# Where an MLP block's shared products are added, which engine empties a turning block, and from which pool a chunk takes its bank, in a two-layer fp32 decoder on Trainium2

## The chip, the cores and the metric

The kernel runs on one core of one Trainium2 chip. Its metric is the time of one execution in device microseconds. TensorE (PE) does the matmuls into PSUM, VectorE (DVE) and ScalarE (ACT) read PSUM and work on SBUF, GpSimd (POOL) here issues the DMAs that add to their destination, and SyncE (SP) issues the loads. Each engine takes its instructions in order and waits on semaphores.

## The reference

Two layers on x of 512 tokens by 1024, in fp32. The final norm follows the second.

```python
h = rmsnorm(x, g_mix)
z = h @ w_in            # attention q, k, v | retention q, k, v, g | gate_a | gate_b
A = sliding-window attention, window 128, 8 query heads on 2 kv heads, rotary, sinks
B = chunkwise retention, 4 heads, rms norm per head, swish gate
x = x + (sigmoid(gate_a) * (A @ w_a) + sigmoid(gate_b) * (B @ w_b)) @ w_out
h2 = rmsnorm(x, g_mlp)
x = x + square(relu(h2 @ w_up)) @ w_down        # 1024 -> 4096 -> 1024
out = rmsnorm(x, g_final)                        # after layer 2
```

## The kernel before

**Products.** Every fp32 operand is split into a high and a low part that TensorE can multiply (`hi` by ACT at L308, `lo` by DVE at L309), and each product is three matmuls, high by high, high by low, low by high (`products`, L354 to L356). A matmul has 128 weights by 512 or 256 columns.

**Weights.** They stream in units of 128 x 1024 through five `raw` buffers (`raw_tile`, L170). SP issues the loads four units ahead, and a unit is split three units before its matmuls (`unit`, `split_until`). For some units DVE first adds two loaded halves (L267 for `pair`, L290 for `block`). Which units are needed and when is a fixed list; the order of all instructions is laid out by a scheduler when the program is built.

**The mix part of a layer** multiplies xh, xl (the split input) by `w_in` in chunks of 128 columns. A `group` (L400) computes four chunks at once, here k, v, q(0), q(1), and then come q(2) and q(3) by `chunk` (L388, called at L652 and L653), each into a bank of PSUM, after which `rotate` (L566 to L572, ACT and DVE) reads the bank. PSUM has eight banks: five in the pool `ps_mm`, three in `ps_aux`. Between the parts POOL also sums blocks of weights in DRAM with accumulating DMAs (`sum_steps`).

**The MLP part** runs over eight blocks of 512 hidden columns a layer. Both matrix products of a block are computed with seven half-size multiplications in place of eight. `pair` (L1138, called twice a block) makes the hidden values: seven multiplications of twelve 128 x 256 matmuls into three banks a, e, b, with ACT copies between them (L1152, L1154, L1157) and relu, square, split and sums on ACT and DVE. `down` (L1213) makes the block's share of y: seven multiplications of two times twelve 128 x 512 matmuls. Its banks are a[0..1] and c[0..1] from `ps_mm` and b[0..1] from `ps_aux`. In order:

- a: first product; ACT copies a into b.
- c: product, then `into.early(1, 1, m, c[m], -1)`.
- b += product, then `into.early(0, 1, m, b[m], 1)`.
- a += product, `put(0, 0)`; c += product, `put(0, 1)`; b += product, `put(1, 1)` with sign -1; b += product, `put(1, 0)`.

Here (i, j) is a quarter of y (half i of the columns, half j of the tokens) and m one of two 128-token parts. So the quarters (1,1) and (0,1) are the sum of an early share and a later one.

**Where the shares go.** For blocks 0 to 6 `into` is `Adding`. Its `early` and `put` both call `send` (L1274): ACT scales the bank by the token's norm factor into a temporary (L1276), and POOL issues a DMA that adds the temporary to y in DRAM (L1278). That is twelve sends of 256 KB a block, four of `eu` from `early` and eight of `y` from `put`. For block 7 `into` is `Ending`: y's quarters are read back into SBUF (L1292), and DVE adds each share from the bank in place (`add`, L1307); only the early (1,1) shares go by ACT and an accumulating DMA. In layer 0, block 7 is then turned back into x (`turn`, L1329; `carry`, L1354, for the halves i = 1, within the next layer's first group). In layer 1, `put` of block 7 goes on to the final norm: ACT's sum of squares (L1315), DVE's multiplication by the gain (L1316, every part), and when both halves of a token part are there, its scaling by 1/rms, for i = 1 by DVE (L1323), for i = 0 by ACT (L1326), and the stores of the result. The last block of layer 1 uses `down_plain` (L1181), which has no early shares.

All temporaries (`temp`: eu, y, rot, junk and others) share one ring of seven 128 x 512 tiles (L131): a new one waits until the tile seven before it is read for the last time, which for a sent tile is the landing of its DMA.

Of the kernel before, what the change touches and what calls it, by code (L numbers as in the profile page):

```python
# [12 lines left out]
AF = mybir.ActivationFunctionType  # L13
ALU = mybir.AluOpType
# [4 lines left out]
T = 512  # L19
# [95 lines left out]
def decoder(ctx, tc, xT, x_first, w_in, w_a, w_b, w_out, w_up, w_pair, w_down, w_end, tables, decay, band, g_last, out):  # L115
    nc = tc.nc
# [7 lines left out]
    ps_mm = ctx.enter_context(tc.tile_pool(name="ps_mm", bufs=5, space=PSUM))  # L124
    ps_aux = ctx.enter_context(tc.tile_pool(name="ps_aux", bufs=3, space=PSUM))

    def f32(ap):
        return ap.bitcast(F32)

    def temp(name="t"):  # L130
        return tmp.tile([P, T], F32, tag="t", name=name, bufs=7)  # L131

    def big(name, dtype=F32):
        return tmp.tile([P, 2, T], dtype, tag="big", name=name, bufs=6)

    def bank(pool, name):
        return pool.tile([P, T], F32, tag=pool.name, name=name)
# [177 lines left out]
    def unit(name, layer):  # L315
        i = state["next"]
        assert order[i][:2] == (layer, name), (order[i], layer, name)
        state["next"] += 1
        split_until(i + SPLIT + 1)
        return parts.pop(i)  # L320
# [27 lines left out]
    def products(ps, pairs, start, stop, resume=False):  # L348


        n = len(pairs)
        for i, ((ah, al), (bh, bl)) in enumerate(pairs):
            more = {"skip_group_check": True} if resume else {}
            nc.tensor.matmul(ps, ah, bh, start=start and i == 0, stop=False, **more)  # L354
            nc.tensor.matmul(ps, ah, bl, start=False, stop=False, **more)  # L355
            nc.tensor.matmul(ps, al, bh, start=False, stop=stop and i == n - 1, **more)  # L356
# [10 lines left out]
    xs = [(xh[:, k, :], xl[:, k, :]) for k in range(KD)]  # L367
# [4 lines left out]
    def advance(rate=1.0):  # L372

        credit[0] += rate
        while credit[0] >= 1.0:
            credit[0] -= 1.0
            while background:
                try:
                    next(background[0])
                    break  # L380
                except StopIteration:
                    background.pop(0)
# [2 lines left out]
        while background:  # L385
            advance()

    def chunk(name, layer, moving, evacuate, rate=1.0):  # L388

        hi, lo = unit(name, layer)  # L390
        n = len(moving)
        ps = bank(ps_mm, "mm")
        pairs = [((hi[:, k * P : (k + 1) * P], lo[:, k * P : (k + 1) * P]), moving[k]) for k in range(n)]
        advance(rate)
        products(ps, pairs[: n // 2], True, False)
        advance(rate)
        products(ps, pairs[n // 2 :], False, True)
        evacuate(ps)
# [110 lines left out]
    def scaled_input(k, which):  # L509

        split(xh[:, k, :], xl[:, k, :], x[:, k, :], gain[:, which * KD + k : which * KD + k + 1])

    def squared_input(k, which):
        if k == 0:
            acc_of[which] = tmp.tile([P, T], F32, tag="acc", name="acc", bufs=1)
        square_sum(acc_of[which], x[:, k, :], k == 0)
# [32 lines left out]
    def layer_body(layer):  # L549
# [14 lines left out]
        def rotate(ps, tabs, early=False):  # L564
            a, b = temp("rot"), temp("rot2")
            nc.scalar.activation(b[0:64, :], ps[64:128, :], AF.Copy)  # L566
            nc.scalar.activation(b[64:128, :], ps[0:64, :], AF.Copy)
            if early:
                nc.scalar.activation(a, ps, AF.Copy)
            nc.vector.tensor_tensor(a, a if early else ps, tabs[0], ALU.mult)  # L570
            nc.vector.tensor_tensor(b, b, tabs[1], ALU.mult)
            nc.vector.tensor_tensor(a, a, b, ALU.add)  # L572
            return a
# [20 lines left out]
        def beside(g, stack, src):  # L594
            for s in range(2):
                own, other = 64 * s + 32 * g, 64 * s + 32 - 32 * g
                nc.sync.dma_start(f32(stack)[other : other + 32, :], f32(src)[own : own + 32, :])
# [33 lines left out]
        def put_q(c):  # L631
            def put(ps):
                r = rotate(ps, attn_tabs, layer == 0 and c < 2)
                if c % 2 == 0:
                    qlo[:] = [big("qlo")]
                lo = qlo[0][:, c % 2, :]
                for g in range(N_KV):
                    nc.scalar.activation(q_s[g][:, c, :], r, AF.Copy)
                nc.vector.tensor_tensor(lo, r, f32(q_s[0][:, c, :]), ALU.subtract)
                for g in range(N_KV):  # L640
                    beside(g, q_s[g][:, c, :], lo)

            return put
# [6 lines left out]
            {0: squares, 1: rms_mix.prepare, 2: stats} if layer == 0 else {0: carried.pop(), 2: rms_mix.prepare, 3: stats},  # L650
        )
        chunk("w_in", layer, xs, put_q(2))  # L652
        chunk("w_in", layer, xs, put_q(3))  # L653
        turn_v()

        a_t = [slots.four() for _ in range(2)]
# [187 lines left out]
        class Head:  # L844


            def __init__(self, h):
                self.h = h
# [110 lines left out]
        for u in range(4):  # L959
            hi, lo = unit("w_a", layer)  # L960
            for j in range(2):
                c = 2 * u + j
                ps = bank(ps_mm, "mm")
# [78 lines left out]
        last = layer == DEPTH - 1  # L1042
        y = dram.tile([P, NB, D], F32, name=f"y{layer}")
# [7 lines left out]
        factor, negative = (columns[:, i * NB : (i + 1) * NB] for i in range(2))  # L1051
        if last:
# [3 lines left out]
            last_gain = gain_tile[:, 0:2, :]  # L1056
# [199 lines left out]
        class Adding:  # L1256


            def __init__(self, e):
                self.e = e  # L1260

            def last_but_one(self):
                pass
# [2 lines left out]
                pass  # L1266

            def early(self, i, j, m, ps, sign):
                self.send(i, j, m, temp("eu"), ps, sign, last or self.e > 0)

            def put(self, i, j, m, ps, sign):
                self.send(i, j, m, temp("y"), ps, sign, last or self.e > 0 or j == 1)

            def send(self, i, j, m, t, ps, sign, add):  # L1274
                block = 2 * j + m
                nc.scalar.activation(t, ps, AF.Copy, scale=(factor if sign > 0 else negative)[:, block : block + 1])  # L1276
                how = {"accum_op": ALU.add} if add else {}
                nc.gpsimd.dma_start(y[:, block, i * T : (i + 1) * T], t, **how)  # L1278

        class Ending:  # L1280


            def __init__(self):
                self.y, self.done = {}, set()
                for i, j in ((1, 1), (0, 1), (0, 0), (1, 0)):
                    if last:
                        two = x[:, 4 * j + 2 * i : 4 * j + 2 * i + 2, :]
                    elif i == 0:
                        two = late_box[0][:, 2 * j : 2 * j + 2, :]
                    else:  # L1290
                        two = big("y")
                    nc.gpsimd.dma_start(two, y[:, 2 * j : 2 * j + 2, i * T : (i + 1) * T])  # L1292
                    for m in range(2):
                        self.y[i, j, m] = two[:, m, :]
# [13 lines left out]

            def put(self, i, j, m, ps, sign):
                block = 2 * j + m  # L1310
                self.add(i, j, m, ps, (factor if sign > 0 else negative)[:, block : block + 1])
                if last:
                    v = self.y[i, j, m]
                    first, total, both = (sq[:, n * NB + block : n * NB + block + 1] for n in range(3))
                    nc.scalar.activation(temp("junk"), v, AF.Square, accum_out=both if i else first)  # L1315
                    nc.vector.tensor_tensor(v, v, last_gain[:, i, :], ALU.mult)  # L1316
                    if not i:
                        nc.vector.tensor_scalar(first, first, 1.0 / D, EPS, ALU.mult, ALU.add)
                        return
                    nc.scalar.activation(total, both, AF.Sqrt, bias=first, scale=1.0 / D)  # L1320
                    nc.vector.reciprocal(total, total)
                    v = self.y[1, j, m]
                    nc.vector.tensor_scalar(v, v, total, None, ALU.mult)  # L1323
                    nc.sync.dma_start(out[:, block, T:], v)
                    v = self.y[0, j, m]
                    nc.scalar.activation(v, v, AF.Copy, scale=total)  # L1326
                    nc.scalar.dma_start(out[:, block, :T], v)
# [24 lines left out]
                    carried.append(self.carry)  # L1352

            def carry(self):  # L1354
                for half in range(2):
                    for j in (1, 0):
                        self.turn(1, j, half, ps_aux)
                    for k in (4 + 2 * half, 5 + 2 * half):
                        scaled_input(k, g_mix + 2)
                for k in range(KD):  # L1360
                    squared_input(k, g_mix + 2)
                    nc.sync.dma_start(spill[:, k, :], x[:, k, :])
                late_box[0] = late_tile(F32R)
                slots.add(late_box[0])
# [200 lines left out]
```

## Time and profile before

| | |
|---|---|
| median of three executions | 1502.52 us (1497.24 to 1502.98) |
| profiled execution | 1501.42 us |
| its span, first to last instruction | 1499.7 us |
| mean granted TensorE clock | 0.997 |
| PE busy | 1471.8 us, 98% |
| DVE busy | 1044.3 us, 70% |
| ACT busy | 940.9 us, 63% |
| POOL busy | 239.7 us, 16% |
| data moved by DMA | 286.25 MB |

The profile is of one execution. Its page gives each engine's busy time, the span in 40 slices, the DMA queues, the chain of work that ended last, the costliest groups of instructions with what ended the idle time before them, and the DMAs with their time from issue to landing. In a row such as `PE mm L354 <- ACT eu L1154` the left side waited and the right side released it; names are those of the program's tiles. Views of the trace cut the same records by stretch of time, by waiting engine or by engine in order of time; the prediction quotes the rows that it uses. Times in rows count from the span's start.

### The profile page before, as it was taken

The page shows a single profiled execution, that of the slowest core. Times are in us where ns is not written, and L with a number is a line of the kernel's source. Part 1 is how long each engine was busy: PE and PEld are TensorE (multiplying, and loading weights), DVE is VectorE, ACT ScalarE, POOL GpSimd, SP SyncE. Part 2 cuts the span into 40 slices and gives each one's busy share as a digit, 9 for nine tenths or more (in the row PEclk, how much of TensorE's full clock was granted, in tenths as well). Part 3 has the DMA queues.
Part 4 walks back from the last instruction along what each step waited for, and adds up shares of the span by engine and source line. Part 5 has one row for each costly group of instructions (what it writes and reads, how often), then busy time and mean ns, then how long its engine had stood idle before and what let it go on. Part 6 is the DMA issues. An engine that isn't in the chain of part 4 may idle for free.

```text
span 1499.7 us, 21303 instructions
## 1 busy us (share of the span) xinstructions
PE 1471.8 (98%) x7787; PEld 1265.7 (84%) x7787; DVE 1044.3 (70%) x1589; ACT 940.9 (63%) x1551; POOL 239.7 (16%) x334
## 2 busy tenths in 40 slices
PE   9999999999999999999999999999999999999997
PEld 7888888888889999998778888888888789888885
DVE  6878568654677777776977775677447677777665
ACT  7657355532568888887755563555325778877775
POOL 0101121101002222223001011111000212222230
PEclk9999999999999999999999999999999999999999
DMA  7654997668227888888836579876443488888883
GB/s 257 189 169 113 303 256 185 185 179 223 92 72 220 211 215 218 223 213 230 290 100 182 147 207 273 223 205 155 140 121 110 122 205 213 210 219 211 218 205 126
DMA packets 100472, 286.25 MB, mean 191 GB/s; under 512 B 11664, under 2 KB 11792, under 8 KB 96528
## 3 DMA queue, kind: packets, MB, share of 16 engines
q0 software_dynamic: 38832, 114.31, 36.3%
q1 hardware_dynamic: 60816, 169.27, 33.5%
q8 instruction: 61, 1.00, 0.3%
q10 hardware_dynamic: 720, 1.31, 0.2%
q14 instruction: 43, 0.35, 0.1%
HBM read 231.37 MB, written 113.77 MB: 230 GB/s over the span
## 4 chain that ended last, share of the span: by engine, by line
PE 87%; DMA 6%; ACT 3%; DVE 2%; issue 2%; DVEq 0%; ACTq 0%
PE mm L354 23%; PE mm L355 23%; PE mm L356 23%; DMA raw<-w_down_in 3%; DMA raw<-w_pair_in 2%; PE rv L354 2%; PE rv L356 2%; PE rv L355 2%; PE b L354 2%; PE b L355 2%; PE b L356 2%; DVE lo L309 1%; PE score L705 1%; ACT hi L308 1%; PE pT L670 1%
## 5 line engine op out<-in xcount | busy, mean ns | idle before, releaser
L308 ACT ACTIVATE hi<-raw 128x1024 fp32r<-128x1024 f32 (+1 forms) x363 | 369.8, 1020 | 324.4 <-PE mm L355 195.4
L309 DVE TENSOR_TENSOR lo<-raw,hi 128x1024 fp32r<-128x1024 f32 (+1 forms) x364 | 424.5, 1170 | 201.9 <-ACT hi L308 199.8
L354 PE MATMUL mm<-xh,hi 128*128 128x512 f32 (+1 forms) x1008 | 358.4, 359 | 14.4 <-ACT eu L1154 9.5
L355 PE MATMUL mm<-xl,hi 128*128 128x512 f32 (+1 forms) x1008 | 356.9, 356 | 0.0
L356 PE MATMUL mm<-xh,lo 128*128 128x512 f32 (+1 forms) x1008 | 356.2, 356 | 0.7 <-DVE lo L309 0.7
L354 PE MATMUL mm<-r,hi 128*128 128x256 f32 (+1 forms) x736 | 238.7, 324 | 0.5 <-ACT mm L1152 0.5
L356 PE MATMUL mm<-r,lo 128*128 128x256 f32 (+1 forms) x736 | 238.9, 325 | 0.0
L355 PE MATMUL mm<-r,hi 128*128 128x256 f32 (+1 forms) x736 | 238.8, 324 | 0.0
L354 PEld LDWEIGHTS mm<-xh,hi 128*128 128x128 f32 x1008 | 190.7, 189 | 44.2 <-ACT eu L1154 12.5
L356 PEld LDWEIGHTS mm<-xh,lo 128*128 128x128 f32 x1008 | 190.7, 189 | 26.2 <-DVE lo L309 0.9
L355 PEld LDWEIGHTS mm<-xl,hi 128*128 128x128 f32 x1008 | 191.0, 189 | 25.5 <-DVE xl L365 0.2
L354 PEld LDWEIGHTS mm<-r,hi 128*128 128x128 f32 x736 | 139.8, 190 | 13.7 <-ACT mm L1152 0.7
L355 PEld LDWEIGHTS mm<-r,hi 128*128 128x128 f32 x736 | 139.8, 190 | 13.1
L356 PEld LDWEIGHTS mm<-r,lo 128*128 128x128 f32 x736 | 139.8, 190 | 11.3
L1278 POOL DMA_DIRECT2D y<-eu x56 | 47.3, 851 | 387.7 <-ACT eu L1276 383.4
L1278 POOL DMA_DIRECT2D y<-y x112 | 98.1, 1257 | 66.4 <-DMA y<-eu 35.5
L355 PE MATMUL mm<-lo,r 128*128 128x512 f32 x272 | 104.2, 392 | 0.0
L356 PE MATMUL mm<-hi,r 128*128 128x512 f32 x272 | 100.7, 390 | 0.0
L354 PE MATMUL mm<-hi,r 128*128 128x512 f32 x272 | 97.8, 393 | 0.2
L267 DVE TENSOR_TENSOR raw<-raw 128x512 f32<-128x512 f32 x56 | 38.5, 688 | 67.6 <-DMA raw<-sums_up 54.1
L354 PE MATMUL b<-hi,r 128*128 128x512 f32 x180 | 70.5, 392 | 1.6 <-DVE y L1307 1.6
L355 PE MATMUL b<-lo,r 128*128 128x512 f32 x180 | 70.3, 390 | 0.0
(262 smaller groups left out, 2314.3 us busy)
## 6 DMA issues: line engine op xcount, KB each, us to landing
raw<-w_in_in SPq DMA_DIRECT2D x89, 512.0 KB, 5.5
sums_down<-w_down_in POOLq DMA_DIRECT2D x30, 1024.0 KB, 11.3
y<-y POOLq DMA_DIRECT2D x120, 256.0 KB, 7.9
sums_up<-w_pair_in POOLq DMA_DIRECT2D x56, 512.0 KB, 9.8
raw<-w_down_in SPq DMA_DIRECT2D x45, 512.0 KB, 8.7
raw<-w_pair_in SPq DMA_DIRECT2D x84, 256.0 KB, 4.2
raw<-sums_down SPq DMA_DIRECT2D x30, 512.0 KB, 9.1
y<-eu POOLq DMA_DIRECT2D x58, 256.0 KB, 5.8
```

The lines of the kernel that those rows point to most:

```text
L267: nc.vector.tensor_tensor(raws[i][:, at], last[:, LEFT], last[:, RIGHT], ALU.add)
L308: nc.scalar.activation(hi[:, at], raw[:, at], AF.Copy)
L309: nc.vector.tensor_tensor(lo[:, at], raw[:, at], f32(hi[:, at]), ALU.subtract)
L354: nc.tensor.matmul(ps, ah, bh, start=start and i == 0, stop=False, **more)
L355: nc.tensor.matmul(ps, ah, bl, start=False, stop=False, **more)
L356: nc.tensor.matmul(ps, al, bh, start=False, stop=stop and i == n - 1, **more)
L670: nc.tensor.transpose(pt[:, i * P : (i + 1) * P], sm[:, at : at + P], ident)
L705: nc.tensor.matmul(ps[:, g * w : (g + 1) * w], q_s[g][:, c, at], part[:, keys], start=i == 0, stop=i == 1)
L1278: nc.gpsimd.dma_start(y[:, block, i * T : (i + 1) * T], t, **how)
```

## The change

Four things are changed, two in the MLP blocks, one in the mix part and one at the end of the kernel. Lines below are those of the kernel before.

- `Adding`: `early` now evacuates a bank with ACT into a temporary and keeps it (`kept`). When `put` comes to a quarter that has a kept tile, DVE multiplies the bank by the factor and adds the kept tile in one instruction, in place, and that sum is sent. Quarters without a kept tile go by ACT as before. A block has eight sends in place of twelve, eight ACT evacuations in place of twelve, and four new DVE instructions. Whether a send adds no longer depends on j.
- `Ending` of layer 0 (the turning block): the late shares of the quarter (1,1) are evacuated by ACT into two temporaries (`aside`), and `carry` adds them to y on DVE before the turns; `carry` now turns j = 0 before j = 1.
- `chunk` has a parameter for the pool of its bank, and q(3) takes its bank from `ps_aux`.
- `Ending` of layer 1: for the halves i = 1 the multiplication by the gain and the scaling by 1/rms become one DVE instruction; the halves i = 0 are as before.

```diff
--- before.py
+++ after.py
@@ -385,11 +385,11 @@
         while background:
             advance()
 
-    def chunk(name, layer, moving, evacuate, rate=1.0):
+    def chunk(name, layer, moving, evacuate, rate=1.0, pool=ps_mm):
 
         hi, lo = unit(name, layer)
         n = len(moving)
-        ps = bank(ps_mm, "mm")
+        ps = bank(pool, "mm")
         pairs = [((hi[:, k * P : (k + 1) * P], lo[:, k * P : (k + 1) * P]), moving[k]) for k in range(n)]
         advance(rate)
         products(ps, pairs[: n // 2], True, False)
@@ -650,7 +650,7 @@
             {0: squares, 1: rms_mix.prepare, 2: stats} if layer == 0 else {0: carried.pop(), 2: rms_mix.prepare, 3: stats},
         )
         chunk("w_in", layer, xs, put_q(2))
-        chunk("w_in", layer, xs, put_q(3))
+        chunk("w_in", layer, xs, put_q(3), pool=ps_aux)
         turn_v()
 
         a_t = [slots.four() for _ in range(2)]
@@ -1257,7 +1257,7 @@
 
 
             def __init__(self, e):
-                self.e = e
+                self.e, self.kept = e, {}
 
             def last_but_one(self):
                 pass
@@ -1266,22 +1266,33 @@
                 pass
 
             def early(self, i, j, m, ps, sign):
-                self.send(i, j, m, temp("eu"), ps, sign, last or self.e > 0)
+                self.kept[i, j, m] = self.evacuated(j, m, temp("eu"), ps, sign)
 
             def put(self, i, j, m, ps, sign):
-                self.send(i, j, m, temp("y"), ps, sign, last or self.e > 0 or j == 1)
-
-            def send(self, i, j, m, t, ps, sign, add):
+                t = self.kept.pop((i, j, m), None)
+                if t is not None:
+                    nc.vector.scalar_tensor_tensor(t, ps, self.scale(j, m, sign), t, ALU.mult, ALU.add)
+                else:
+                    t = self.evacuated(j, m, temp("y"), ps, sign)
+                self.send(i, j, m, t, last or self.e > 0)
+
+            def scale(self, j, m, sign):
                 block = 2 * j + m
-                nc.scalar.activation(t, ps, AF.Copy, scale=(factor if sign > 0 else negative)[:, block : block + 1])
+                return (factor if sign > 0 else negative)[:, block : block + 1]
+
+            def evacuated(self, j, m, t, ps, sign):
+                nc.scalar.activation(t, ps, AF.Copy, scale=self.scale(j, m, sign))
+                return t
+
+            def send(self, i, j, m, t, add):
                 how = {"accum_op": ALU.add} if add else {}
-                nc.gpsimd.dma_start(y[:, block, i * T : (i + 1) * T], t, **how)
+                nc.gpsimd.dma_start(y[:, 2 * j + m, i * T : (i + 1) * T], t, **how)
 
         class Ending:
 
 
             def __init__(self):
-                self.y, self.done = {}, set()
+                self.y, self.aside = {}, {}
                 for i, j in ((1, 1), (0, 1), (0, 0), (1, 0)):
                     if last:
                         two = x[:, 4 * j + 2 * i : 4 * j + 2 * i + 2, :]
@@ -1308,19 +1319,24 @@
 
             def put(self, i, j, m, ps, sign):
                 block = 2 * j + m
-                self.add(i, j, m, ps, (factor if sign > 0 else negative)[:, block : block + 1])
+                scale = (factor if sign > 0 else negative)[:, block : block + 1]
+                if not last and (i, j) == (1, 1):
+                    t = self.aside[m] = temp("eu")
+                    nc.scalar.activation(t, ps, AF.Copy, scale=scale)
+                else:
+                    self.add(i, j, m, ps, scale)
                 if last:
                     v = self.y[i, j, m]
                     first, total, both = (sq[:, n * NB + block : n * NB + block + 1] for n in range(3))
                     nc.scalar.activation(temp("junk"), v, AF.Square, accum_out=both if i else first)
-                    nc.vector.tensor_tensor(v, v, last_gain[:, i, :], ALU.mult)
                     if not i:
+                        nc.vector.tensor_tensor(v, v, last_gain[:, i, :], ALU.mult)
                         nc.vector.tensor_scalar(first, first, 1.0 / D, EPS, ALU.mult, ALU.add)
                         return
                     nc.scalar.activation(total, both, AF.Sqrt, bias=first, scale=1.0 / D)
                     nc.vector.reciprocal(total, total)
                     v = self.y[1, j, m]
-                    nc.vector.tensor_scalar(v, v, total, None, ALU.mult)
+                    nc.vector.scalar_tensor_tensor(v, v, total, last_gain[:, 1, :], ALU.mult, ALU.mult)
                     nc.sync.dma_start(out[:, block, T:], v)
                     v = self.y[0, j, m]
                     nc.scalar.activation(v, v, AF.Copy, scale=total)
@@ -1352,8 +1368,11 @@
                     carried.append(self.carry)
 
             def carry(self):
+                for m in range(2):
+                    v = self.y[1, 1, m]
+                    nc.vector.tensor_tensor(v, v, self.aside[m], ALU.add)
                 for half in range(2):
-                    for j in (1, 0):
+                    for j in range(2):
                         self.turn(1, j, half, ps_aux)
                     for k in (4 + 2 * half, 5 + 2 * half):
                         scaled_input(k, g_mix + 2)
```

## The prediction

> **What bounds the kernel now.** I read the page's head first, then what TensorE (PE) waits for, then the same by stage, and the chain of waits only where a stage loses time.
>
> ```profile
> span 1499.7 us, 21303 instructions
> PE 1471.8 (98%) x7787; PEld 1265.7 (84%) x7787; DVE 1044.3 (70%) x1589; ACT 940.9 (63%) x1551; POOL 239.7 (16%) x334
> q0 software_dynamic: 38832, 114.31, 36.3%
> ```
>
> PE is busy 1471.8 of 1499.7 us, so the most that any reshuffling of other engines can give is 1499.7 − 1471.8 = 27.9 us, and only where PE stands still. The page names who makes it stand still:
>
> ```profile
> PE mm L354 <- ACT eu L1154: 9.5, 9, 2.0
> PE mm L354 <- DVE rot L570: 2.8, 1, 2.8
> PE mm L354 <- ACT xh L364: 2.0, 2, 1.3
> PE b L354 <- DVE y L1307: 1.6, 1, 1.6
> ```
>
> Columns: total us, times, longest. The first row is the copy of a `pair` product to SBUF, the second the rotation of layer 1's queries, the last two the hand-over from layer 0 to layer 1. By stage (stretch, length, then PE, PEld, DVE, ACT, POOL busy, granted clock, DMA share, GB/s):
>
> ```profile
> 555.00:595.00 40.00, 40.00 (x257) 36.35 (x256) 30.25 (x39) 32.85 (x54) 10.52 (x12) 1.00 0.85 211
> 715.00:740.00 25.00, 22.63 (x115) 18.65 (x113) 23.93 (x33) 15.99 (x26) 3.53 (x4) 1.00 0.86 283
> 760.00:780.00 20.00, 17.17 (x74) 13.93 (x73) 12.92 (x19) 11.42 (x18) 0.00 (x0) 0.91 0.27 84
> 1420.00:1465.00 45.00, 41.86 (x269) 37.74 (x268) 30.82 (x39) 34.98 (x58) 12.86 (x15) 1.00 0.86 229
> ```
>
> One of layer 0's MLP blocks (first row) has PE busy 40.00 of 40.00 us. There the removed DMAs and ScalarE (ACT) copies can bring nothing by themselves. The change can gain only in the other three places and in the tail, and it can lose in all fourteen `Adding` blocks.
>
> **The change, part by part.**
>
> *The chunk's bank (770 us).* This is the surest term.
>
> ```profile
> 770.46 0.39 PE L356 MATMUL mm<-xh,lo 128*128 128x512 f32 x1
> 772.94 0.68 DVE L570 TENSOR_TENSOR rot<-mm,tab 128x512 f32<-128x512 f32 x1
> 773.67 0.80 PE L354 MATMUL mm<-xh,hi 128*128 128x512 f32 x1 [2.83 <-DVE rot L570]
> 776.40 0.45 PE L354 MATMUL mm<-xh,hi 128*128 128x512 f32 x1
> 776.91 0.39 PE L356 MATMUL mm<-xh,lo 128*128 128x512 f32 x1
> 777.14 0.39 PE L354 MATMUL mm<-xh,hi 128*128 128x512 f32 x1
> ```
>
> q(3) waits 2.83 us for a bank of `ps_mm` that VectorE (DVE) frees at L570. Then the six matmuls from 773.67 to 776.40 take 2.73 us, where six at the later pitch (777.14 − 776.91 = 0.23) take 1.38; the granted clock of this window is 0.91. So the stall costs 2.83 + 1.35 = 4.2 us. By the changed program's order the bank that q(3) gets from `ps_aux` was last used by a turn of the carry, long done by then; its weights are split three units ahead; and DVE (12.92 of 20) and DMA (share 0.27) have room. I take −4.2. Bounds: 0, if the wait moves to the next chunk, and −4.2. [...]
>
> *The turning block and the carry (700–740 us).* ACT takes the two (1,1) results (about 0.69 us each by L1276's rows below), DVE loses two L1307 there and gains two adds later, beside attention input work. Of the 1.6 us that PE waits for DVE at L1307 something goes; but DVE is busy 23.93 of 25 us there, so what is queued on it next (turning adds, xh, xl) becomes the late one, and the two adds come back behind it at 0.68 each (as L1316 below). Bounds: −3.6 (both hand-over rows, 1.6 + 2.0) to +1.4 (two adds on the path). I take −1.
>
> *The Adding blocks, DVE and ACT.*
>
> ```profile
> L1276 ACT ACTIVATE y<-b,columns 128x512 f32<-128x512 f32 x56 | 38.9, 695 | 27.4 <-DMA y<-y 12.4 <-DMA y<-eu 11.3 <-PE b L356 2.5
> L1307 DVE SCALAR_TENSOR_TENSOR y<-b,columns,y 128x512 f32<-128x512 f32 x4 | 3.0, 740 | 0.0
> ```
>
> Per block ACT loses 4 × 0.695 = 2.8 us and DVE gains 4 × 0.74 = 3.0 on top of 30.25 of 40. Where they fall decides:
>
> ```profile
> 568.19 0.68 DVE L362 TENSOR_TENSOR r<-sums,r 128x512 fp32r<-128x512 f32 x1
> 569.62 1.22 DVE L309 TENSOR_TENSOR lo<-raw,hi 128x1024 fp32r<-128x1024 f32 x1 [0.75 <-ACT hi L308]
> 575.13 0.69 DVE L267 TENSOR_TENSOR raw<-raw 128x512 f32<-128x512 f32 x1 [4.28 <-DMA raw<-sums_up]
> ```
>
> The put of (0,1) is due near 568.2, that of (1,1) near 571.3, and DVE idles 0.75 and 4.28 us at just these places. The second pair is free. In front of the `lo` at 569.62 two adds of 0.66 each (two L1307 end to end) do not fit 0.75 us, so `lo` starts about 0.5 late; it was done 0.9 before its matmul by my count of PE's order (estimate), so 0.4 remains. Layer-0 cost: 0, bounds 0 and 14 × 0.35 = +5 (one whole add of 0.74 late, less the 0.4).
>
> *The eight DMAs.* 114.31 MB took 36.3% of 1499.7 = 544 us of all 16 engines, so a 256 KB send takes 0.262/114.31 × 544 = 1.25 us; four fewer are 5.0 us of the 34 (0.85 × 40) that a block moves. It matters where PE waits on ACT:
>
> ```profile
> 1280.23 6.95 DMA raw<-w_pair_in
> 1287.60 0.28 issue
> 1287.88 1.83 DVE lo L309 x2
> 1289.73 9.60 DMA raw<-w_down_in
> 1299.45 0.92 issue
> 1300.38 0.37 ACT eu L1154
> ```
> ```profile
> PE mm L354 <- ACT eu L1154: 7.3, 7, 2.0
> ```
>
> (The last row is the same waits view, cut to 1185–1470 us.) In layer 1's blocks ACT stands in order behind the split of a w_down half whose load takes 9.60 us; the eu copy that PE wants is queued behind it. Two of the four removed sends lie well before that load, the other two join its crowd, and those that stay are issued as before. Bounds: 0 and −7.3. With a third of the removed work in the load's own stretch I take −2.5.
>
> *The longer-lived tiles.* Temporaries come from one ring of seven. The last evacuation of (1,0) now takes the place of the kept (0,1) tile, whose send must have landed. The waits of before at this place:
>
> ```profile
> 578.38 0.69 ACT L1276 ACTIVATE y<-b,columns 128x512 f32<-128x512 f32 x1 [0.77 <-DMA y<-y]
> 579.66 0.39 ACT L1154 ACTIVATE eu<-mm 128x256 f32<-128x256 f32 x1 [0.60 <-DMA y<-y]
> ...
> y<-y POOLq DMA_DIRECT2D x120, 256.0 KB, 7.9
> ```
>
> The new send goes out near 569.2 and lands after 7.9 us (median) at 577.1, before ACT wants the place at 578.4. So 0, with a price below as a rival. Behind that evacuation stand the next block's eu copy and split.
>
> *The tail.* Eight L1316 and four scalings become four L1316 and four fused ones.
>
> ```profile
> 1490.89 0.68 DVE L1316 TENSOR_TENSOR x<-x,late 128x512 f32<-128x512 f32 x1
> 1491.49 0.48 DVE L1323 TENSOR_SCALAR x<-x,sq 128x512 f32<-128x512 f32 x1
> 1491.88 0.15 DVE L1321 RECIPROCAL sq<-sq 128x1 f32<-128x1 f32 x1
> 1491.96 0.73 DVE L1307 SCALAR_TENSOR_TENSOR x<-mm,columns,x 128x512 f32<-128x512 f32 x1
> 1492.61 0.68 DVE L1316 TENSOR_TENSOR x<-x,late 128x512 f32<-128x512 f32 x1
> ```
>
> Start to start, L1316 holds DVE 0.60, the scaling 0.39, a two-tensor scalar op 0.65. Each of four blocks saves 0.60 + 0.39 − 0.65 = 0.34; DVE runs end to end here and ends the kernel, so −1.2 of the possible −1.4 (bounds 0 and −1.4).
>
> **Sum.** −4.2 − 1 − 2.5 − 1.2 = −8.9. The profiled execution took 1501.42 us (span 1499.7 and 1.7 around it), 1.1 under the median 1502.52 of the three runs shown. 1501.42 − 8.9 = 1492.5; with the 1.1 back, 1493.6, say **1493.5**.
>
> **The rivals.**
>
> 1. *The relief clears layer 1's waits.* The 9.60 us load needs to land only 2.0 us sooner (the longest wait), and 5.0 us of engine time left the block. Against it: layer 0 has the same share (0.85) and no such wait, so the share alone doesn't make it. Then −7.3 in place of −2.5: 1493.5 − 4.8 = 1488.7, and 1486 if the hand-over's 3.6 goes as well. [...]
>
> 2. *Slower: the ring.* If the kept tile's send lands later than the median, ACT waits at the last (1,0) evacuation, and with it the next `pair`'s eu copy. PE has about 1.5 us of slack there (estimate from the order), so it decides from a landing of about 9.5 us. POOL's other transfers show up to 11.3:
>
> ```profile
> sums_down<-w_down_in POOLq DMA_DIRECT2D x30, 1024.0 KB, 11.3
> ```
>
> At 11.3 it costs 1.8 us in each of 14 blocks, +25; layer 1's −2.5 goes too: 1493.5 + 2.5 + 25 = 1521. It is slower than before from a landing of about 10.0 on (14 × 0.5 = 7, against the 6.4 that the other terms give). For it: 0.77 and 0.60 us of such waits exist already. Against: those transfers are four times as large, and there are four fewer sends.
>
> 3. *The bank change only moves the wait.* If the next chunk (gate) meets the same full `ps_mm`, PE stops one chunk later, for the same 2.8 us with its slow clock: 1493.5 + 4.2 = 1497.7. Against: that chunk comes 24 matmuls, 24 × 0.23 = 5.5 us, later, and DVE's L570 releases the first bank at 773.6.
>
> 4. *`lo` comes late by a whole add in every Adding block* (+5), and layer 1 gains nothing (+2.5): 1501.0, no change.
>
> **How the numbers follow.** Half a per cent, 7.5 us, is about what a measurement of this kernel can tell from no change; the bounds are 1495.0 and 1510.0. Forecast (1489–1495): 0.42. Rival 1 (1484–1489): 0.18. Rival 3, or the small gains missing one by one: 0.15. Rival 4: 0.11. Rival 2: 0.14, of which I put 0.03 short of 1510 and 0.11 above. So faster 0.42 + 0.18 = 0.60; same 0.15 + 0.11 + 0.03 = 0.29; slower 0.11. The range of 8 in 10 runs from 1485 (part of rival 1 below it) to 1506 (rival 2 above it).
>
> **What would show it.** The row "DVE rot L570" gone from PE's waits and a clock near 1.00 in 760–780: the bank. "ACT eu L1154" between 1185 and 1470: near 5 us for my forecast, near 0 for rival 1, well over 9.5 with "DMA y<-eu" ahead of ACT for rival 2. PE waits on `lo` L309 at a put of (0,1) for rival 4. The time from the last matmul to the end shorter by 1.2. In layer 0's blocks PE still 40.00 of 40.00; if not, the forecast is wrong.

## The result and the profile after

The changed kernel takes 1484.3 us (median of four, 1482.02 to 1484.4), the kernel before 1501.78 us in the same comparison. The ratio is 0.9891 (95% interval 0.9871 to 0.9911), so 17.5 us, 1.1%, faster. The forecast was 1493.5, 9.0 us below the median that it started from; the measured time lies 0.7 us below the low end of the range, and 1.7 us below the lower figure of rival 1 (1486).

The head of the changed kernel's page:

```profile
span 1482.5 us, 21265 instructions
PE 1467.6 (99%) x7787; PEld 1266.1 (85%) x7787; DVE 1081.5 (73%) x1641; ACT 912.7 (62%) x1497; POOL 191.2 (13%) x278
...
q0 software_dynamic: 30768, 99.63, 30.6%
```

DVE has 37 us more work, ACT 28 us less, the sends' queue 14.7 MB less. None of the three bounded the kernel; PE stands still less. The view of what PE waits for:

```profile
PE turn L1350 <- DVE y L1318: 1.6, 1, 1.6
PE mm L355 <- DVE xl L365: 1.2, 1, 1.2
...
PE mm L354 <- ACT xh L364: 1.0, 2, 0.6
PE mm L356 <- DVE lo L309: 0.6, 1, 0.6
```

All nine waits on `ACT eu L1154` (9.5 us) are gone, and the wait on `DVE rot L570`. What is left at the top lies in the hand-over between the layers (L1350 is in `turn`, L1318 in `add`; L1334 and L1307 before). The same by stage, with the columns as in the prediction:

```profile
555.00:595.00 40.00, 40.00 (x258) 36.56 (x257) 33.21 (x43) 30.87 (x50) 7.04 (x8) 1.00 0.67 185
715.00:740.00 25.00, 23.01 (x115) 18.70 (x114) 23.92 (x34) 17.38 (x27) 3.49 (x4) 1.00 0.84 279
760.00:780.00 20.00, 20.00 (x89) 16.54 (x89) 14.92 (x22) 13.98 (x23) 0.00 (x0) 1.00 0.30 95
1420.00:1465.00 45.00, 45.00 (x279) 40.66 (x278) 27.61 (x35) 28.04 (x46) 10.15 (x12) 1.00 0.66 182
```

Layer 0's window was full and stays full, although DVE has three more us of work in it and the DMA share falls from 0.85 to 0.67. The 20 us around q(3) are full now at clock 1.00 (17.17 at 0.91 before). The stretch in layer 1's last blocks goes from 41.86 of 45 to full.

A full window hides short stalls, which the view of waits doesn't list either. The start of `down`'s first matmul into b shows them, block by block. From the second block of a layer to the seventh, these starts lay 39.28 to 39.89 us apart in layer 0 before and 39.75 to 40.81 in layer 1; now they are 39.25 apart in both. So layer 0's blocks too had lost 1.5 us in all.

What I had not looked at is POOL. In the groups of instructions, its sends before the change:

```profile
L1278 POOL DMA_DIRECT2D y<-y x112 | 98.1, 1257 | 66.4 <-DMA y<-eu 35.5 <-ACT hi L308 13.4 <-ACT y L1276 12.6
```

Ahead of `y` sends POOL stood still 35.5 us for the landing of `eu` sends: the second share of a quarter adds to the same place in DRAM as the first, so here it is not issued before the first has landed, and the sends behind it in POOL's order left only then (five at 1286.71 below). One block in time, POOL and then SP in the kernel before:

```profile
1277.26 0.86 POOL L1278 DMA_DIRECT2D y<-eu  x1 [5.18 <-ACT eu L1276]
1278.49 0.86 POOL L1278 DMA_DIRECT2D y<-eu  x1 [0.36 <-issue]
1279.88 1.76 POOL L1278 DMA_DIRECT2D y<-y  x2 [0.53 <-ACT y L1276]
1283.98 0.86 POOL L1278 DMA_DIRECT2D y<-y  x1 [2.33 <-DMA y<-eu]
1286.71 4.45 POOL L1278 DMA_DIRECT2D y<-y  x5 [1.87 <-DMA y<-eu]
...
1289.73 0.33 SPq L284 DMA_DIRECT2D raw<-w_down_in  x1
```

and in the changed kernel:

```profile
1273.45 2.54 POOL L1289 DMA_DIRECT2D y<-eu  x2
1276.68 0.86 POOL L1289 DMA_DIRECT2D y<-y  x1 [0.70 <-ACT y L1284]
1278.04 0.86 POOL L1289 DMA_DIRECT2D y<-y  x1 [0.50 <-ACT y L1284]
...
1280.57 0.33 SPq L284 DMA_DIRECT2D raw<-w_down_in  x1
```

Before, five sends leave in the 3.0 us ahead of the w_down load and the 1.4 us behind it. After, only one leaves in the 3.0 us ahead of it, and none behind it. In layer 1's other blocks it is four or five before, and one or two after. While this load was under way (9.6 us before, 7.3 after), the sends' queue moved 1.16 MB before and 0.87 MB after. The median landing of that load, and of its sister from `sums_down`, falls from 8.7 and 9.1 us to these rows of the changed page:

```profile
raw<-w_down_in SPq DMA_DIRECT2D x45, 512.0 KB, 6.9
...
raw<-sums_down SPq DMA_DIRECT2D x30, 512.0 KB, 7.1
y<-eu POOLq DMA_DIRECT2D x58, 256.0 KB, 8.2
```

Counted from the start of `down`'s first matmul into b, a block's first w_down load landed after 26.1 to 26.5 us in layer 0 before, after 26.6 to 27.6 in layer 1, and lands after 24.2 to 25.3 in both now (second block to seventh). This is how layer 0 could have the crowd and hardly a wait: its loads came just early enough.

That these waits stand behind the load can be read in ACT's order. ACT and then PE in the kernel before:

```profile
1299.41 1.06 ACT L308 ACTIVATE hi<-raw 128x1024 fp32r<-128x1024 f32 x1 [0.67 <-DMA raw<-w_down_in]
1300.38 0.36 ACT L1154 ACTIVATE eu<-mm 128x256 f32<-128x256 f32 x1
...
1300.79 0.39 PE L354 MATMUL mm<-xh,hi 128*128 128x256 f32 x1 [0.85 <-ACT eu L1154]
```

ACT stood idle until the load had landed. It is so at seven of the nine waits, 7.1 of the 9.5 us (six times for w_down, once for w_end in the last block). Of the other two, one (0.55 us) comes behind ACT's waits for sends, and one (1.80 us, at 712) behind a split that waited for PE.

### The profile page after: what moved, and what is told of

It is laid out like the page before. It is cut to its first block, busy times and chain, and to the rows that moved or that the text cites. A ratio compares the mean times of both kernels' runs of the same rounds, so it can differ in the third digit from the quotient of the medians.

```text
span 1482.5 us, 21265 instructions
## 1 busy us (share of the span) xinstructions
PE 1467.6 (99%) x7787; PEld 1266.1 (85%) x7787; DVE 1081.5 (73%) x1641; ACT 912.7 (62%) x1497; POOL 191.2 (13%) x278
## 4 chain that ended last, share of the span: by engine, by line
PE 95%; DVE 2%; ACT 2%; DMA 1%; issue 1%; SPq 0%; ACTq 0%; DVEq 0%
PE mm L354 25%; PE mm L356 25%; PE mm L355 25%; PE b L354 2%; PE b L355 2%; PE b L356 2%; PE rv L354 2%; PE rv L356 2%; PE rv L355 2%; PE score L705 1%; PE pT L670 1%; PE r L355 1%; PE r L356 1%; PE r L354 1%; ACT hi L308 1%
## 5 line engine op out<-in xcount | busy, mean ns | idle before, releaser
L1289 POOL DMA_DIRECT2D y<-eu x56 | 62.0, 1345 | 371.3 <-DVE eu L1274 371.3
L354 PE MATMUL b<-hi,r 128*128 128x512 f32 x180 | 70.4, 391 | 0.0
L1289 POOL DMA_DIRECT2D y<-y x56 | 55.6, 1007 | 111.8 <-ACT y L1284 106.5
L356 PE MATMUL b<-hi,r 128*128 128x512 f32 x180 | 67.8, 389 | 0.0
## 6 DMA issues: line engine op xcount, KB each, us to landing
sums_down<-w_down_in POOLq DMA_DIRECT2D x30, 1024.0 KB, 10.4
```

The costliest lines, as they stand in the source:

```text
L1289: nc.gpsimd.dma_start(y[:, 2 * j + m, i * T : (i + 1) * T], t, **how)
```

## The experiments

My theory after the result, L: four fewer sends, and none late, land the weight loads sooner, so that ACT's split, and the `pair` copy queued behind it, come in time. Rivals: W, ACT simply has 2.8 us less to do in a block; R, the ring of seven temporaries, which made ACT wait for landings, is what got relief.

### Each part alone

`adding_only` is the kernel before with the new `Adding`; `bank_only` is it with q(3)'s bank alone:

```diff
-        chunk("w_in", layer, xs, put_q(3))
+        chunk("w_in", layer, xs, put_q(3), pool=ps_aux)
```

> The kernel before with the Adding part of the change alone. If the kept tiles carry what the changed kernel won beyond the bank and the tail, PE's waits on ACT eu L1154 (9.5 us before) go to near 0 and the wait on DVE rot L570 stays at 2.8: about 1501.8 - 11 = 1491. If the parts only win together (the rival to that), the L1154 waits stay over 5 us and the time is over 1496.

> The kernel before with q(3)'s bank from the other pool alone. My term: the wait on DVE rot L570 gone, granted clock 1.00 in 760 to 780 us, 1501.8 - 4.2 = 1497.6; L1154 stays near 9.5 us. Rival: the wait moves to the next chunk, no gain, 1501.8.

`adding_only` took 1487.09 us (0.9902, 0.9873 to 0.9931). No wait on L1154 is left, and the wait on `DVE rot L570` stays at 2.8. `bank_only` took 1494.25 us (0.9960, 0.9945 to 0.9976); its 20 us around q(3) are full at clock 1.00, and L1154 is at 6.6. So `Adding` alone gives 13.8 us (10.4 to 19.1), the larger part of the 17.5. The bank gives 6.0 by the interval's middle (3.6 to 8.3), which holds the 4.2 that the place itself explains. The two add up to 2.3 us more than the whole, which is within their intervals; that both won some of the same L1154 waits (6.6 in place of 9.5 with the bank alone) is possible, but not shown.

### More traffic again: spare_sends, spare_static

The first sends the kept tiles to a spare tensor as well, and puts the sum into a tile of its own:

```diff
-                self.kept[i, j, m] = self.evacuated(j, m, temp("eu"), ps, sign)
+                t = self.kept[i, j, m] = self.evacuated(j, m, temp("eu"), ps, sign)
...
+                nc.gpsimd.dma_start(spare[:, 2 * j + m, i * T : (i + 1) * T], t, **how)
...
-                    nc.vector.scalar_tensor_tensor(t, ps, self.scale(j, m, sign), t, ALU.mult, ALU.add)
+                    t = temp("y")
+                    nc.vector.scalar_tensor_tensor(t, ps, self.scale(j, m, sign), kept, ALU.mult, ALU.add)
```

> The changed kernel with its DMA traffic put back: the kept tiles are also sent to a spare tensor in DRAM that nothing reads, and the sum goes to a tile of its own, so that a block has twelve sends and fourteen temporaries again, while ACT still evacuates eight and DVE adds four. Theory L (fewer sends, so the weight loads land sooner): loads of w_down_in back from 6.9 to about 8.7 us, L1154 waits back to 7 to 10 us, about 1484.3 + 9 = 1493. Theory W (ACT has 2.8 us less to do in a block): waits stay near 0, about 1484.3. Theory R (the ring of seven temporaries makes ACT wait for landings): ACT's waits on DMA y come back (31 us in before) and with them the PE waits, 1493, but the loads' landing may stay near 7.

It took 1536.61 us (1.0235, 1.0209 to 1.0261), a result that no theory had. Its waits, of PE and then of DVE:

```profile
PE mm L356 <- DVE lo L309: 30.4, 25, 2.0
...
DVE y L1278 <- DMA spare<-eu: 42.1, 13, 3.7
```

DVE's new tile takes the ring's place of a tile that is still being sent, so the landing wait has moved to DVE, and the splits of weights queue behind it. It tells nothing between L and R: with all twelve sends back the w_down loads landed after 6.0 us, but in a kernel that was held up elsewhere. It shows what a landing wait can cost, as in rival 2 of the prediction, though there it is ACT that waits: 42.1 us of DVE's time came with 52 us of the kernel's.

The second takes the ring out of it: the four extra sends read a tile that stands still.

```diff
+                mark = small.tile([P, 1], F32, tag="mark", name="mark", bufs=2)
+                ins = nc.gpsimd.tensor_copy(mark, t[:, 0:1])
...
+                with tc.issue_after(ins.ins):
+                    nc.gpsimd.dma_start(spare[:, 2 * j + m, i * T : (i + 1) * T], f32(xh[:, 2 * j + m, :]), **how)
```

> The changed kernel with four more sends of 256 KB a block, added into a spare tensor that nothing reads, issued by POOL when each early tile is there (a one-column copy on POOL orders them). Their source is a tile that stands still (xh), so neither the ring of temporaries nor ACT's or DVE's work changes; what comes back is the DMA traffic alone, twelve sends a block. Theory L (the DMA engines' relief lands the weight loads sooner): w_down_in back from 6.9 to 8.7 us, PE's L1154 waits between 1185 and 1470 back to 5 to 8 us, about 1484.3 + 7 = 1491. Theories W and R (ACT's work, or the ring): waits near 0, about 1484 to 1486.

It took 1490.93 us (0.9937, 0.9917 to 0.9956): the sends, with the POOL work to issue them, take back 6.6 of the 17.5 us. The number is the one that I gave for L, but the place is not: between 1185 and 1470 no wait on the eu copy came back. ACT's waits, then the landings:

```profile
ACT y L1290 <- DMA y<-eu: 35.6, 12, 3.3
```
```profile
raw<-w_down_in SPq DMA_DIRECT2D x45, 512.0 KB, 7.9
...
y<-eu POOLq DMA_DIRECT2D x58, 256.0 KB, 10.3
```

The loads are 1.0 us slower than in the changed kernel, and a send now lands after 10.3 us, so the last evacuation of (1,0) waits for the kept tile's landing. That is rival 2's place, past the 9.5 us that it had named. Seven of PE's waits on `hi` come some 2 us behind such a wait of about 3 us; no wait of PE comes behind a late w_down load. Rival 2 would have priced 10.3 at 0.8 us in each of 14 blocks, 11 us; all of the added traffic cost 6.6. So the same 114.31 MB as before, issued at other times, do not bring L's waits back. The blocks are some 0.5 us longer than the changed kernel's, though, which gives each load that much more time.

### ACT's work: early_dve, act_back

```diff
+                if early:
+                    nc.vector.tensor_scalar(t, ps, scale, None, ALU.mult)
+                else:
+                    nc.scalar.activation(t, ps, AF.Copy, scale=scale)
```

> The changed kernel with the Adding of before, twelve sends, but the four early evacuations done by DVE in place of ACT, so that only ACT's work falls by 2.8 us a block. Theory W: L1154 waits near 0, about 1484.3 to 1486. Theories L and R: the waits stay at 7 to 10 us, about 1484.3 + 9 = 1493.

```diff
                 if t is not None:
+                    nc.scalar.activation(ps, ps, AF.Copy)
                     nc.vector.scalar_tensor_tensor(t, ps, self.scale(j, m, sign), t, ALU.mult, ALU.add)
```

> The changed kernel in which ACT first copies each shared bank onto itself in PSUM before DVE adds it, so that ACT handles twelve banks a block again with eight sends and the ring as changed. Theory W (ACT's 2.8 us a block): L1154 waits back to 5 to 8 us, about 1491. Theories L and R: L1154 waits near 0; DVE's add comes some 0.6 us later, so PE may wait for b at 0.3 us here and there: 1484 to 1488.

`early_dve` took 1508.16 us (1.0051, 1.0034 to 1.0068) and `act_back` 1503.87 (1.0020, 1.0005 to 1.0035): both missed, since each made a chain of its own. In the first, L1154 falls to 3.2 us although w_down loads land after 8.7 as before and POOL's landing waits are longer (54.7 us in place of 35.5). But its blocks take 40.6 to 41.7 us, so a load may come later, and its five waits on L1154 all stand behind ACT's waits for sends; it isn't a clean win for W. In the second PE waits 10.2 us for b at DVE's add, which comes behind ACT's extra pass, and L1154 is at 2.8. Of that, 1.5 us stand behind the w_end load of layer 1's last block, and none behind w_down: with twelve passes of ACT and eight sends the waits behind w_down do not come back, though here too the blocks are longer (40.2 to 41.3 us). What speaks most against W is the trace of before: ACT stood idle until the load landed (nine times for w_down, 6.9 us in all), so it was not short of time there. Neither run excludes a share of W.

### The ring: ring5_after, ring8_before

```diff
-        return tmp.tile([P, T], F32, tag="t", name=name, bufs=7)
+        return tmp.tile([P, T], F32, tag="t", name=name, bufs=5)
```

> The changed kernel with a ring of five temporaries in place of seven: ten temporaries a block in five places is as tight as the fourteen in seven of before. Theory R (waits for a landing in front of ACT): ACT's waits on DMA y come back (31 us in before, none after), and PE's L1154 waits with them, 1490 to 1500 or more since four places hold kept tiles. Theories L and W: some waits of ACT, but PE's stay below 3 us, 1484 to 1488.

It took 1513.39 us (1.0088, 1.0058 to 1.0118). PE's largest wait and ACT's:

```profile
PE mm L354 <- ACT eu L1154: 20.1, 13, 2.2
...
ACT y L1284 <- DMA y<-eu: 22.1, 23, 2.0
ACT y L1284 <- DMA y<-y: 20.6, 10, 3.4
ACT eu L1154 <- DMA y<-eu: 16.9, 12, 2.5
```

Its w_down loads land after 5.6 us. So the ring alone can make just these PE waits. Whether it made them before is asked by giving the kernel before one tile more, bufs=8 (for its place, the attention's masking is left out and one kind of small tile has four buffers in place of six):

> The kernel before with a ring of eight temporaries in place of seven, and nothing else of the change. The place for it comes from the attention mask: its tile is left out and the mask is read from another tile (so the attention's masking is left out). Twelve sends, twelve ACT evacuations. Theory R (waits for a send's landing in front of ACT): ACT's 31 us of waits on DMA y fall below 8, since each was under 1.3 us and the place is now free one send earlier; PE's L1154 waits fall from 9.5 to below 3; about 1501.5 - 7 = 1494.5. Theory L (the loads share the DMA engines with the sends): ACT's waits on y may fall, but ACT then waits for w_down_in (9 us landing as before) and L1154 stays at 7 to 10 us; about 1501.

It took 1500.49 us (0.9998, 0.9980 to 1.0017), no change. PE's wait, then ACT's:

```profile
PE mm L353 <- ACT eu L1153: 8.4, 8, 1.9
...
ACT hi L308 <- DMA raw<-w_pair_in: 15.6, 9, 3.3
ACT hi L308 <- DMA raw<-w_down_in: 7.2, 8, 1.8
...
ACT eu L1153 <- DMA y<-y: 2.5, 8, 0.5
```

ACT's waits for sends' landings are down to 2.5 us, against these before:

```profile
ACT y L1276 <- DMA y<-y: 12.4, 13, 1.2
...
ACT y L1276 <- DMA y<-eu: 11.3, 16, 1.1
...
ACT eu L1154 <- DMA y<-y: 7.4, 13, 0.6
```

yet PE waits 8.4 us at the same copy (L1153 here), 6.6 of it behind a weight load and 1.8 behind the split at the hand-over. R falls for this kernel: 28.6 of ACT's 31.1 us of landing waits went without any effect on the time; what PE waits for stands behind the loads.

### Which sends: keep11, keep01

Both have ten sends, ten ACT evacuations and two DVE adds a block; they differ in the quarter that is kept.

```diff
+                if (i, j) == (1, 1):
+                    self.kept[i, j, m] = t
+                else:
+                    self.send(i, j, m, t, last or self.e > 0)
```

> The changed kernel that keeps only the early tiles of (1,1); those of (0,1) are sent as before: ten sends a block, ten evacuations by ACT, two adds by DVE. If the relief is a matter of amount (L or W), about half of the 9.5 us of L1154 waits come back: 1488 to 1490. If it has a threshold, 1484 to 1485 (the half is enough) or 1493 (it is not).

> The changed kernel that keeps only the early tiles of (0,1); those of (1,1) are sent as before: ten sends a block. These are sent first, long before the w_down loads, so if the place of a send matters more than the count, it should do better than the variant that keeps (1,1) (1494.6): near 1486. If only the count matters, 1494 to 1495.

`keep11` took 1494.63 us (0.9957, 0.9938 to 0.9975), `keep01` 1486.92 (0.9917, 0.9891 to 0.9943): 7.7 us apart at the same count. I had meant this as a test of the place alone. POOL and SP in `keep11`, then in `keep01`:

```profile
1285.75 0.86 POOL L1293 DMA_DIRECT2D y<-y  x1 [0.37 <-ACT y L1288]
...
1286.66 0.33 SPq L284 DMA_DIRECT2D raw<-w_down_in  x1
```
```profile
1277.69 0.86 POOL L1293 DMA_DIRECT2D y<-y  x1 [0.49 <-ACT y L1288]
...
1281.34 0.33 SPq L284 DMA_DIRECT2D raw<-w_down_in  x1
```

With (0,1) sent twice within a few us, POOL waits 18.1 us in all for landings and the last sends leave just ahead of the load; with (1,1) sent twice, the first is long landed, POOL waits for no landing of an `eu` in these blocks, and 3.7 us lie between the last send and the load. But the loads hardly differ: w_down lands after 7.9 us in `keep11` and 7.6 in `keep01`. What differs is ACT. In `keep11` it waits for the landing of sends whose places in the ring it needs; in `keep01` it has no such wait:

```profile
ACT y L1288 <- DMA y<-eu: 33.2, 27, 2.4
...
ACT y L1288 <- DMA y<-y: 12.0, 12, 1.6
```

PE's waits at L1154 are 1.5 us in `keep01`; in `keep11` PE waits 4.8 us at `hi` instead, and each of these eleven waits comes behind three of ACT's. ACT and then PE, one block of `keep11`:

```profile
1280.24 0.69 ACT L1288 ACTIVATE y<-mm,columns 128x512 f32<-128x512 f32 x1 [1.93 <-DMA y<-eu]
...
1284.71 0.69 ACT L1288 ACTIVATE y<-b,columns 128x512 f32<-128x512 f32 x1 [0.91 <-DMA y<-y]
1285.29 1.57 ACT L308 ACTIVATE hi<-raw 128x512 fp32r<-128x512 f32 x2
...
1286.91 0.39 PE L354 MATMUL mm<-xh,hi 128*128 128x256 f32 x1 [0.61 <-ACT hi L308]
```

So the waits that PE shows here come by the ring, as R and rival 2 have it, and not by the load. The pair does not test whether a send's place ahead of a load matters.

Not tried: the kernel before with its twelve sends and evacuations and only POOL's landing wait taken away. How much of the loads' relief is the count of the sends, and how much their place, therefore stays open.

### The turning block: turn_undone, turn_dma

`turn_undone` is the changed kernel with the turning block of before. `turn_dma` adds the (1,1) shares by an accumulating DMA in place of DVE:

```diff
-                    t = self.aside[m] = temp("eu")
+                    t = temp("eu")
                     nc.scalar.activation(t, ps, AF.Copy, scale=scale)
+                    nc.gpsimd.dma_start(self.y[i, j, m], t, accum_op=ALU.add)
```

> The changed kernel with the turning block as before (DVE adds (1,1) from the bank, no aside tiles, turns j = 1 first). If that part of the change gains the 0.7 us by which the hand-over stalls are shorter, 1485.0; if that gain comes from the sends (the 710 us wait on L1154) and the part itself costs, 1483 (adding_only shows 4.6 us of stalls there with the old turning block, the changed kernel 5.7).

> The changed kernel in which the turning block's (1,1) shares, evacuated by ACT, are added to y by an accumulating DMA, as its early shares are, in place of two DVE adds in the carry. DVE is the bound there (23.92 of 25 us): two adds of 0.68 fewer give 1484.3 - 1.3 = 1483. Rival: the carry's turns wait for the DMA's landing, 8 us, 1485 to 1488.

`turn_undone` took 1482.52 us (0.9881, 0.9859 to 0.9903), `turn_dma` 1484.00 (0.9893, 0.9873 to 0.9912). The hand-over with the old turning block, from the windows of `turn_undone`, and then of the changed kernel:

```profile
700.00:760.00 60.00, 56.47 (x311) 48.22 (x310) 48.31 (x67) 38.16 (x60) 5.54 (x7) 1.00 0.77 262
```
```profile
700.00:760.00 60.00, 55.80 (x312) 47.58 (x311) 48.31 (x66) 38.82 (x60) 6.89 (x8) 1.00 0.77 262
```

PE stands still 0.7 us less with the old form. The times agree in sign, but their intervals overlap. `turn_undone` is the fastest version seen, faster than both kernels by its median. `turn_dma` met its rival in the trace, where PE waits 4.3 us at the turns for the DMA's landing, but not in its time, which is that of the changed kernel.

## Why the prediction was right or wrong

- **The bank: right.** −4.2 forecast; 2.83 us of waiting and a clock of 0.91 became 20.00 of 20.00 at 1.00. The next chunk met no full pool. `bank_only` confirms the place; its time agrees, with a wide interval.
- **The tail: right.** −1.2 forecast. From the start of the last matmul to the span's end it was 1499.7 − 1490.03 = 9.7 us, and is 1482.5 − 1474.12 = 8.4:

```profile
1490.03 0.39 PE L356 MATMUL mm<-hi,r 128*128 128x512 f32 x1
```
```profile
1474.12 0.39 PE L356 MATMUL mm<-hi,r 128*128 128x512 f32 x1
```

- **DVE's four adds and the longer-lived tiles: right at nothing.** Layer 0's blocks are 39.25 us apart, `lo` costs PE 0.6 us in the whole kernel, and ACT waits at no evacuation for a landing. Rivals 2 and 4 did not come. `spare_static` shows how near rival 2 was: two us more of landing (10.3 in place of 8.2), and the wait is there. What was wrong is the remark that one full window leaves nothing to gain in layer 0: its blocks gave 1.5 us.
- **The turning block: wrong in sign, by the trace.** −1 forecast. The hand-over did get about 1 us better (54.84 to 55.80 us of PE in 700 to 760), but by another part: L1154's wait of 1.80 us at 712 is gone. It is gone in `adding_only` too, so it belongs to `Adding`; no load stands behind it, but a split that ACT had ahead of the copy in its order and that waited for PE. The turning block itself costs some 0.7 us (`turn_undone`). The two adds that come back on DVE hold it from 733.27 to 734.47, and the L1318 that PE's turn waits for (1.6 us) comes behind them: the positive end of my bounds.
- **The eight DMAs: the step that failed.** I took −2.5 of −7.3 because two of the four removed sends "join its crowd, and those that stay are issued as before". Neither holds. In the block shown, the removed sends had all landed when the load was issued: POOL's wait for the last of them ended by 1286.71, and the load went out at 1289.73. Its crowd are the `y` sends that stay, and these are not issued as before. I had read how long a send occupies the DMA engines, but not what POOL waits for before it issues. With each quarter sent once, POOL's 35.5 us of landing waits are gone and most of the sends that stay leave well before the load. All 7.3 us went.

The outcome was thus that of rival 1, by another way than the engine time that it counted. I gave it 0.18, for the reason that layer 0 has the same DMA share without such waits. But that share (0.85, and 0.86 in layer 1's last blocks) did not tell when the one load lands that is waited for: in layer 0 it landed 0.1 to 1.5 us earlier in the block than in layer 1. In the block shown the sends' queue moved 1.16 MB beside the load in 9.6 us before, and 0.87 MB in 7.3 us after, about 0.12 MB a us both times. `spare_static`, with four more sends, had w_down land after 7.9 us in place of 6.9; how sends slow a load, no run here shows. I had asked only where the removed sends lie beside the load, and not when those that stay would leave.

The profiled difference is 17.2 us (1501.42 to 1484.25). Cut at the starts of `down`'s first matmul into b, the changed kernel is 2.0 us later at the first block, and then wins 3.5 us over layer 0's blocks, 3.3 from there to layer 1's first block, 8.4 over layer 1's blocks and 4.0 from the last block to the end. That start lies at 442.7 to 444.9 us in all the runs, with and without the change, so I take the 2.0 for chance. The 3.3 hold the bank's 4.2, less about 0.9 for the turning block (`turn_undone` wins 4.3 there); the 4.0 hold the tail's 1.3 and the 2.0 us wait on L1154 behind the w_end load. In the blocks, L1154's listed waits are less than what went; the rest are stalls too short for the view.

## What to carry to other kernels

Before pricing the removal of a DMA, read what its queue waits for: two accumulating sends to one place in DRAM were here a chain through a landing (5.8 us for the first, by the page of before), and what stood behind the second in POOL's order left later with it (35.5 us of POOL's waits). Then look at which load these late sends fall on and at when that load is needed, and not at the mean share of the DMA engines. A long list of one engine's waits is no evidence by itself: one more buffer took away 28.6 of ACT's 31.1 us before and the time stayed, while in `keep11` 45.2 us of the same kind stood ahead of PE's waits. The instruction just ahead of the one that is waited for tells which case it is.

## What the runs showed of the hardware

A clock drop does not follow each PE wait of this length. `ring8_before` has the same 2.83 us wait for q(3)'s bank, and its window shows no drop, where the kernel before and `adding_only` had 0.91:

```profile
760.00:780.00 20.00, 17.17 (x80) 13.99 (x79) 11.92 (x17) 11.69 (x17) 0.00 (x0) 1.00 0.25 80
```

The 1.35 us that I added for it are thus there in some executions only; three are too few to say how often. Why a wait of 2.83 us came with the lower clock in two runs and not in a third, no run here shows.
